# Out projection and values: the squares for the next norm run two slices later behind the residual rows' accumulating DMAs

## The chip, the cores and the metric

The kernel runs on one core of a Trainium2 chip. The time is the device time of one execution in microseconds, the median of several runs. The engines named below are PE (matrix products, with PEld for its weight loads), DVE (vector), ACT (scalar and activation), POOL (general) and SP, which here only issues DMAs. Each engine works through its own list of instructions strictly in order. A wait in that list holds up everything behind it on the same engine.

## The reference, cut to what matters

One transformer-like layer on 2048 tokens of width 1024, in float32. Between the sub-layers stand RMS norms, one behind each sub-layer before the residual is added (post) and one ahead of the next (pre):

```
y = concatenate([ya, yh]) @ w_out          # out projection
h = h + rms_norm(y, g_mix_post)            # residual row h1
u = rms_norm(h, g_x_pre)                   # only its 1/rms is needed as a factor of the scores
y = cross_attention(u, m, wq, wk, wv, wo)  # scores, softmax, values
h = h + rms_norm(y, g_x_post)              # residual row h2
u = rms_norm(h, g_ffn_pre)                 # input of the feed-forward
y = (silu(u @ w_gate) * (u @ w_up)) @ w_down
h = h + rms_norm(y, g_ffn_post)
```

So each row of the out projection and of the values is normed twice: its squares are summed, it is scaled, the residual is added, and the squares of the sum are summed again for the next norm.

## The kernel before, in words

The head of the program (input projection, windowed attention, the recurrence, and the folding of the cross-attention weights into two 1024 x 1024 matrices) takes the first 790 us and isn't touched. Then `phases` runs a chain of jobs, each a product of 2048 tokens with 1024 x 1024 matrices: the out projection (`mixed_block`), the scores (`score_block`), the values (`value_block`), gate and up of the feed-forward (`hidden_blocks`) and three parts of the down projection (`down_block`).

A job of these consists of eight blocks of 256 tokens (n = 0, 2, ... 14, counted in 128-token rows). A block multiplies by a scheme with seven instead of eight products of halves (`seven`). Each of the seven steps is one slice: 12 matrix products of 128 x 128 by 128 x 512, since every float32 operand is split into a high and a low part (`products`, lines 1032 to 1034). The two first and the two last blocks of a job run as pairs, slice by slice in turn; the middle four run one after the other. The token operands S are made from loaded tiles by `streamed` and `split2` (ACT line 896 or POOL line 898 for the high part, DVE line 899 for the low one) into five rotating buffers. The weight operands T are loaded through `row` tiles and split once per job. A product bank that isn't finished is copied by ACT into a `part` tile (line 1047) before it is used again.

When a quarter of a block (one of two rows of 128 tokens, one half of the width) is done, `out` adds it into a `row` tile (`squared`: DVE line 1391 or ACT line 1393) and sums its squares on ACT (`mean_square`, line 1369, profile name `junk`). What is still to be done with the block's two rows is written as a generator, `after`, which is appended to a list when the block's last slice has been recorded. From then on each slice of later blocks advances each `after` in the list by one `yield`. So a `yield` is one slice of distance in the order in which the program is recorded. A planner then orders each engine's list by its own estimate of times and by the dependencies, so the distance on the chip isn't exactly the recorded one.

In the two jobs of the change, `after` does the following, slice by slice: `rstds` on POOL (lines 1380, 1382, 1384: sum, epsilon, power -0.5), the scaling of each row on DVE (line 1417 or 1489), the residual added by an accumulating DMA issued by POOL (`add`, line 1398), the store of the residual row by SP (line 78, `h_d<-row`: the profile shortens h1_d and h2_d to this name); one slice of pause; the squares of each row's sum, two per row on ACT (`mean_squares`, line 1369); a second `rstds`. The out projection keeps its result in r_x (line 1426), transposes both rows on PE (`transposed`, line 1284, copied by ACT, line 1285) and stores them as h1t. The values scale each row again into a new `row` tile u on DVE (line 1500), transpose that and store it in u_d; for n = 4 and 6 sums of halves are also formed and stored (u_s). The row is transposed from, squared and stored only after the accumulating DMA has landed.

`row` tiles come from one pool of nine; the rows of T, the blocks' rows, u and the rows for the sums of the next job's weights share it.

Of the kernel before, what the change touches and what calls it, by code (L numbers as in the profile page):

```python
# [48 lines left out]
class Layer:  # L49
# [1350 lines left out]
    def mixed_block(self, n):  # L1400
        nc = self.nc
        y, ss = {}, []

        def out(i, j, a, b):
            if not y:
                ss.append(self.small("q_s", 4))
                if not n:
                    self.g_mix_post = self.gain(self.I["g_mix_post"])
            if i not in y:
                y[i] = self.row_tile()  # L1410
            self.squared(y[i][:, j * 512:(j + 1) * 512], a, b, ss[0][:, 2 * i + j:2 * i + j + 1])

        def after():
            r = self.rstds(ss[0])
            s2 = self.small("q_s", 4)
            for i in range(2):
                nc.vector.scalar_tensor_tensor(y[i], y[i], r[:, i:i + 1], self.g_mix_post, ALU.mult, ALU.mult)
                self.add(y[i], self.I["x"], n + i)
                self.store(self.h1_d[(n + i) * P:(n + i + 1) * P, :], y[i])
                yield  # L1420
            yield
            for i in range(2):
                self.mean_squares(y[i], i, s2)
                yield
            r = self.rstds(s2)
            nc.gpsimd.tensor_scalar(self.r_x[:, n:n + 2], r, 1.0, None, ALU.mult)
            yield
            for i in range(2):
                self.store(self.h1t_d[n + i], self.transposed(y[i], y[i]))
                yield  # L1430

        return self.tokens(self.y_d, n), out, after, None

    def score_block(self, n):
# [35 lines left out]
    def value_block(self, n):  # L1470
        nc = self.nc
        y, ss = {}, []

        def out(i, j, a, b):
            if not y:
                ss.append(self.small("q_s", 4))
            if i not in y:
                y[i] = self.row_tile()
                if n == 0 and len(y) == 1:
                    self.g_x_post = self.gain(self.I["g_x_post"])  # L1480
                    self.g_ffn_pre = self.extra_tile()
                    self.load(self.g_ffn_pre, self.I["g_ffn_pre"][0:1, :].broadcast_to([P, D]))
            self.squared(y[i][:, j * 512:(j + 1) * 512], a, b, ss[0][:, 2 * i + j:2 * i + j + 1])

        def after():
            r = self.rstds(ss[0])
            s2 = self.small("q_s", 4)
            for i in range(2):
                nc.vector.scalar_tensor_tensor(y[i], y[i], r[:, i:i + 1], self.g_x_post, ALU.mult, ALU.mult)
                self.add(y[i], self.h1_d, n + i)  # L1490
                self.store(self.h2_d[(n + i) * P:(n + i + 1) * P, :], y[i])
                yield
            yield
            for i in range(2):
                self.mean_squares(y[i], i, s2)
                yield
            r = self.rstds(s2)
            u = [self.row_tile() for _ in range(2)]
            for i in range(2):
                nc.vector.scalar_tensor_tensor(u[i], y[i], r[:, i:i + 1], self.g_ffn_pre, ALU.mult, ALU.mult)  # L1500
                yield
            o = []
            yield
            for i in range(2):
                tv = self.transposed(u[i], u[i])
                self.store_transposed(self.u_d, n + i, tv)
                if 4 <= n < 8:
                    o.append(self.row_tile().rearrange("p (k t) -> p k t", k=KT))
                    self.load(o[i], self.u_d[:, :, (n + i - 4) * P:(n + i - 3) * P].rearrange("k p t -> p k t"))
                yield  # L1510
            for i in range(len(o)):
                tv = u[i].rearrange("p (k t) -> p k t", k=KT)
                s = self.row_tile().rearrange("p (k t) -> p k t", k=KT)
                with self.behind():
                    nc.vector.tensor_tensor(s[:, 0:4], tv[:, 0:4], o[i][:, 0:4], ALU.subtract)
                    nc.vector.tensor_tensor(s[:, 4:8], tv[:, 4:8], tv[:, 0:4], ALU.subtract)
                yield
                with self.behind():
                    nc.vector.tensor_tensor(o[i][:, 0:4], o[i][:, 0:4], s[:, 4:8], ALU.add)
                    nc.vector.tensor_tensor(o[i][:, 4:8], o[i][:, 4:8], o[i][:, 0:4], ALU.subtract)  # L1520
                at = slice((n + i - 4) * P, (n + i - 3) * P)
                for c, t in enumerate((s[:, 0:4], s[:, 4:8], o[i][:, 0:4], o[i][:, 4:8])):
                    self.store(self.u_s[c][:, :, at], t)
                yield

        return self.tokens(self.pt_d, n), out, after, None

    def hidden_blocks(self, b, f):
# [137 lines left out]
```

## Time and profile before

| what | us |
|---|---|
| median of 3 runs (2600.45 to 2605.1) | 2603.19 |
| the profiled execution | 2603.6 |
| its span | 2601.7 |
| PE busy, share of the span | 2528.0, 97% |
| ACT busy | 1262.0 |
| DVE busy | 1746.0 |
| granted clock of PE, mean | 0.992 |

The span is the time from the first to the last instruction. A matrix product counts as busy from its issue to its end, and products overlap, so a busy share of 97% doesn't say that PE runs at its peak; what a change can win is read from the places where PE sits idle. In the profile's rows a bracket holds the idle time ahead of an instruction on its engine and what ended it. A granted clock below 1 means that PE was throttled for part of a stretch.

### The profile page before, as it was taken

Reading aid. Unit: us, or ns where it says so; the run is one execution under the profiler, and the core shown is the slowest. Engines: PE = TensorE matmul, PEld = TensorE weight load, DVE = VectorE, ACT = ScalarE, POOL = GpSimd, SP = SyncE. Lnnn points to the kernel's source line nnn. Section 1 sums busy time; section 2 is a strip of 40 time slices with the busy share of each in tenths; the row PEclk is TensorE's granted clock in tenths of the full one; section 3 lists DMA queues with packets and bytes.
Section 4 is the critical chain, followed back from the end, with each engine's and each line's share of the span. In section 5 each row is a group of like instructions: output and inputs, shape, how many; then the busy total and the mean of one; then the engine's idle time right before and its main releaser. Section 6 shows DMA issues by size and latency. Waiting matters only on the chain.

```text
span 2601.7 us, 34516 instructions
## 1 busy us (share of the span) xinstructions
PE 2528.0 (97%) x12160; PEld 2115.2 (81%) x12160; DVE 1746.0 (67%) x2773; ACT 1262.0 (49%) x2641; POOL 466.6 (18%) x651
## 2 busy tenths in 40 slices
PE   7989999999998999999999999999999999999998
PEld 6878788878997778888778888888888888888786
DVE  7675578887646568786785555576666656664756
ACT  5463366655654565565563333354333335443543
POOL 4240343320312224223320000000000000000022
PEclk9999999999999999999999999999999999999999
DMA  5434655484875998656984532353456434576798
GB/s 186 143 120 167 208 157 171 131 267 157 279 259 207 289 328 258 221 191 187 302 273 138 167 124 73 105 186 116 167 182 230 147 108 168 174 225 174 232 228 208
DMA packets 286350, 497.88 MB, mean 191 GB/s; under 512 B 20576, under 2 KB 143456, under 8 KB 286176
## 3 DMA queue, kind: packets, MB, share of 16 engines
q1 hardware_dynamic: 275520, 456.87, 52.3%
q0 software_dynamic: 10656, 38.80, 8.0%
q8 instruction: 96, 1.57, 0.2%
q14 instruction: 78, 0.64, 0.1%
HBM read 328.87 MB, written 166.72 MB: 190 GB/s over the span
## 4 chain that ended last, share of the span: by engine, by line
PE 80%; DMA 8%; DVE 4%; issue 3%; POOL 2%; ACT 2%; SPq 0%; DVEq 0%; POOLq 0%; ACTq 0%
PE psm L1032 22%; PE psm L1034 22%; PE psm L1033 22%; PE psg L163 2%; PE psg L164 2%; PE psg L165 2%; DMA row<-in_x_dram 1%; PE pss L1284 1%; DMA row<-h_d 1%; DMA u_d<-row 1%; DMA h_d<-row 1%; DMA x<-in_w_out_dram 1%; ACT junk L1369 1%; DMA pair<-in_x_dram 1%; DMA extra<-qk_d 0%
## 5 line engine op out<-in xcount | busy, mean ns | idle before, releaser
L1032 PE MATMUL psm<-T,S 128*128 128x512 f32 x2664 | 1036.4, 393 | 24.6 <-ACT S L896 13.8
L1033 PE MATMUL psm<-T,S 128*128 128x512 f32 x2664 | 1041.9, 391 | 0.0
L1034 PE MATMUL psm<-T,S 128*128 128x512 f32 x2664 | 1037.3, 392 | 2.6 <-DVE S L899 2.5
L1032 PEld LDWEIGHTS psm<-T,S 128*128 128x128 f32 x2664 | 503.3, 189 | 132.6 <-ACT S L896 15.1
L1034 PEld LDWEIGHTS psm<-T,S 128*128 128x128 f32 x2664 | 502.5, 189 | 109.2 <-DVE S L899 4.8
L1033 PEld LDWEIGHTS psm<-T,S 128*128 128x128 f32 x2664 | 503.2, 189 | 103.3
L896 ACT ACTIVATE S<-sum 128x512 fp32r<-128x512 f32 (+1 forms) x338 | 208.0, 619 | 340.1 <-PE psm L1034 331.7
L899 DVE TENSOR_TENSOR S<-sraw,S 128x512 fp32r<-128x512 f32 (+1 forms) x311 | 214.4, 697 | 224.4 <-ACT S L896 214.9
L899 DVE TENSOR_TENSOR S<-sum,S 128x512 fp32r<-128x512 f32 (+1 forms) x404 | 277.1, 690 | 84.3 <-ACT S L896 66.6
L1047 ACT ACTIVATE part<-psm 128x512 f32<-128x512 f32 x297 | 175.1, 592 | 174.9 <-PE psm L1034 168.0
L896 ACT ACTIVATE S<-sraw 128x512 fp32r<-128x512 f32 (+1 forms) x272 | 166.8, 617 | 154.7 <-PE psm L1034 143.1
L1398 POOL DMA_DIRECT2D row<-y_d x28 | 25.0, 892 | 1131.4 <-DMA sraw<-hid_d 964.8
L1369 ACT ACTIVATE junk<-row 128x512 f32<-128x512 f32 x160 | 99.7, 624 | 121.8 <-DVE row L1391 33.4
L899 DVE TENSOR_TENSOR T<-row,T 128x1024 fp32r<-128x1024 f32 x104 | 123.0, 1190 | 28.7 <-ACT T L896 28.5
L163 PE MATMUL psg<-u,whi 128*128 128x512 f32 x352 | 141.2, 401 | 1.0 <-POOL whi L145 1.0
L165 PE MATMUL psg<-u,wlo 128*128 128x512 f32 x352 | 139.5, 396 | 1.5 <-DVE wlo L146 1.5
L164 PE MATMUL psg<-u,whi 128*128 128x512 f32 x352 | 139.6, 397 | 0.0
L896 ACT ACTIVATE T<-row 128x1024 fp32r<-128x1024 f32 x104 | 105.8, 1027 | 23.7 <-DMA row<-in_w_down_dram 10.9
L146 DVE TENSOR_TENSOR wlo<-raw,whi 128x1024 fp32r<-128x1024 f32 x54 | 68.8, 1275 | 33.2 <-ACT whi L143 26.6
L898 POOL TENSOR_SCALAR S<-sum 128x512 fp32r<-128x512 f32 x66 | 49.0, 742 | 234.7 <-PE psm L1034 141.0
L1550 DVE TENSOR_TENSOR part<-psm,part 128x512 f32<-128x512 f32 x66 | 45.4, 688 | 64.6 <-PE psm L1034 64.5
L1541 DVE TENSOR_TENSOR row<-psm,part 128x512 f32<-128x512 f32 x66 | 45.5, 689 | 57.4 <-PE psm L1034 57.3
(329 smaller groups left out, 3644.3 us busy)
## 6 DMA issues: line engine op xcount, KB each, us to landing
sraw<-in_w_gate_dram SPq DMA_DIRECT2D x44, 512.0 KB, 4.9
sraw<-in_w_up_dram SPq DMA_DIRECT2D x44, 512.0 KB, 4.8
hid_d<-row SPq DMA_DIRECT2D x44, 512.0 KB, 2.7
h_d<-row SPq DMA_DIRECT2D x32, 512.0 KB, 6.9
y_d<-row SPq DMA_DIRECT2D x32, 512.0 KB, 3.6
sraw<-hid_d SPq DMA_DIRECT2D x32, 512.0 KB, 5.2
row<-h_d POOLq DMA_DIRECT2D x30, 512.0 KB, 8.1
row<-y_d POOLq DMA_DIRECT2D x28, 512.0 KB, 7.3
```

Source lines behind the costliest of these rows:

```text
L146: nc.vector.tensor_tensor(lo, raw, f32(hi), ALU.subtract)
L163: nc.tensor.matmul(ps, ah, bh, start=(i == 0), stop=False)
L164: nc.tensor.matmul(ps, ah, bl, start=False, stop=False)
L165: nc.tensor.matmul(ps, al, bh, start=False, stop=(i == n - 1))
L896: self.nc.scalar.activation(hi, raw, AF.Copy)
L898: self.nc.gpsimd.tensor_scalar(hi, raw, 1.0, 1.0, ALU.mult, ALU.mult)
L899: self.nc.vector.tensor_tensor(lo, raw, f32(hi), ALU.subtract)
L1032: nc.tensor.matmul(ps, s[:, 0, k, :], t[:, 0, k, :], start=st, stop=False, **kw)
L1033: nc.tensor.matmul(ps, s[:, 0, k, :], t[:, 1, k, :], start=False, stop=False, **kw)
L1034: nc.tensor.matmul(ps, s[:, 1, k, :], t[:, 0, k, :], start=False, stop=sp, **kw)
L1047: nc.scalar.activation(t, ps, AF.Copy)
L1369: self.nc.scalar.activation(junk, a, AF.Square, scale=float(D) ** -0.5, accum_out=to)
```

## The change

In `mixed_block` and in `value_block` the pause between the slice that issues the second row's residual add and the slice with the first row's squares grows from one `yield` to three. Everything behind it in `after` (squares, second `rstds`, second scaling, transposes, stores of h1t or u) is recorded two slices later. Nothing is added, removed or computed differently. `down_block`, which has a similar pause, stays as it was.

```
@@ mixed_block, after
                 self.add(y[i], self.I["x"], n + i)
                 self.store(self.h1_d[(n + i) * P:(n + i + 1) * P, :], y[i])
                 yield
-            yield
+            for _ in range(3):
+                yield
             for i in range(2):
                 self.mean_squares(y[i], i, s2)
                 yield
@@ value_block, after
                 self.add(y[i], self.h1_d, n + i)
                 self.store(self.h2_d[(n + i) * P:(n + i + 1) * P, :], y[i])
                 yield
-            yield
+            for _ in range(3):
+                yield
             for i in range(2):
                 self.mean_squares(y[i], i, s2)
                 yield
```

More of the change, by code (lines that the diff above doesn't have):

```diff
@@ L1420, in after @@
                 yield
-            yield
+            for _ in range(3):
+                yield
             for i in range(2):
@@ L1492, in after @@
                 yield
-            yield
+            for _ in range(3):
+                yield
             for i in range(2):
```

## The prediction

> **What bounds the kernel now.** I read the page first, then the busy time by windows, then the idle stretches of PE in its timeline, then who waits for what around the line that moves.
>
> ```profile
> span 2601.7 us, 34516 instructions
> PE 2528.0 (97%) x12160; PEld 2115.2 (81%) x12160; DVE 1746.0 (67%) x2773; ACT 1262.0 (49%) x2641; POOL 466.6 (18%) x651
> PE 80%; DMA 8%; DVE 4%; issue 3%; POOL 2%; ACT 2%; SPq 0%; DVEq 0%; POOLq 0%; ACTq 0%
> L1369 ACT ACTIVATE junk<-row 128x512 f32<-128x512 f32 x160 | 99.7, 624 | 121.8 <-DVE row L1391 33.4
> ```
>
> PE carries 80% of the chain, so a change elsewhere counts only where PE waits for it, and through the clock that it finds after a wait. The windows show where that is (columns: PE, PEld, DVE, ACT and POOL busy, granted clock, DMA share, GB/s):
>
> ```profile
> 880.00:900.00 20.00, 17.60 (x79) 14.70 (x80) 11.99 (x15) 11.53 (x28) 6.22 (x11) 0.91 0.92 301
> 920.00:940.00 20.00, 17.06 (x73) 13.78 (x72) 8.81 (x13) 8.92 (x23) 4.76 (x9) 0.91 0.97 287
> 980.00:1000.00 20.00, 17.98 (x84) 14.79 (x84) 16.12 (x20) 10.72 (x26) 11.38 (x17) 0.98 0.88 219
> 1000.00:1020.00 20.00, 20.00 (x94) 16.52 (x93) 16.92 (x25) 13.10 (x33) 6.91 (x11) 0.94 1.00 345
> 1020.00:1170.00 150.00, 150.00 (x723) 125.14 (x722) 123.66 (x226) 91.28 (x213) 34.76 (x48) 1.00 0.60 202
> 1290.00:1310.00 20.00, 17.23 (x67) 13.25 (x66) 15.06 (x18) 13.46 (x27) 5.37 (x8) 0.83 1.01 306
> 1330.00:1350.00 20.00, 15.75 (x68) 12.81 (x68) 16.22 (x20) 12.58 (x28) 5.24 (x8) 0.93 0.96 258
> 1350.00:2601.00 1251.00, 1239.29 (x5473) 1024.56 (x5471) 772.86 (x1137) 506.10 (x895) 51.08 (x69) 1.00 0.53 167
> ```
>
> Scores (1020 to 1170) keep PE full at clock 1.00, and the 1251 us of the feed-forward lose 12 us in all. The holes lie in the two jobs that the diff touches, the out projection (about 790 to 990) and the values (about 1165 to 1345), with the DMA share near 1. PE's idle stretches there, in brackets with the releaser:
>
> ```profile
> 878.70 0.39 PE L1033 MATMUL psm<-T,S 128*128 128x512 f32 x1
> 878.93 0.39 PE L1034 MATMUL psm<-T,S 128*128 128x512 f32 x1
> 882.40 1.34 PE L1284 MATMUL pss<-ident,row 128*128 128x128 f32 x8 [2.40 <-DMA row<-in_x_dram]
> 884.40 0.63 PE L1033 MATMUL psm<-T,S 128*128 128x512 f32 x1
> 884.82 0.63 PE L1034 MATMUL psm<-T,S 128*128 128x512 f32 x1
> 910.21 0.47 PE L1032 MATMUL psm<-T,S 128*128 128x512 f32 x1 [1.39 <-DVE row L1391]
> 930.10 1.26 PE L1284 MATMUL pss<-ident,row 128*128 128x128 f32 x8 [2.94 <-DMA row<-in_x_dram]
> 999.00 1.92 PE L1284 MATMUL pss<-ident,row 128*128 128x128 f32 x8 [2.02 <-ACT row L1285]
> 1281.47 1.06 PE L1284 MATMUL pss<-ident,row 128*128 128x128 f32 x8 [1.42 <-DVE row L1500]
> 1299.94 0.79 PE L1032 MATMUL psm<-T,S 128*128 128x512 f32 x1 [2.65 <-ACT S L896]
> 1347.62 0.79 PE L1032 MATMUL psm<-T,S 128*128 128x512 f32 x1 [4.25 <-ACT S L896]
> ```
>
> Products follow each other every 0.23 us before a hole and every 0.42 us for some time behind it (878.70/878.93 against 884.40/884.82). A slice is 12 products, so 12 x 0.23 = 2.8 us, and a block of 7 slices with its 16 transposes about 21 us.
>
> The six holes other than that at 910.21 have one root: the residual row's accumulating DMA hasn't landed when something in order behind it comes up.
>
> ```profile
> 865.52 0.60 ACT L1393 ACTIVATE row<-psm 128x512 f32<-128x512 f32 x1 [1.31 <-PE psm L1034]
> 882.37 0.63 ACT L1369 ACTIVATE junk<-row 128x512 f32<-128x512 f32 x1 [8.03 <-DMA row<-in_x_dram]
> 886.79 0.62 ACT L1369 ACTIVATE junk<-row 128x512 f32<-128x512 f32 x1
> 907.60 0.63 ACT L1369 ACTIVATE junk<-row 128x512 f32<-128x512 f32 x1 [3.14 <-DMA row<-in_x_dram]
> 912.06 0.62 ACT L1369 ACTIVATE junk<-row 128x512 f32<-128x512 f32 x1
> 930.07 0.63 ACT L1369 ACTIVATE junk<-row 128x512 f32<-128x512 f32 x1 [8.49 <-DMA row<-in_x_dram]
> 935.20 0.62 ACT L1369 ACTIVATE junk<-row 128x512 f32<-128x512 f32 x1
> 1337.67 0.64 ACT L1369 ACTIVATE junk<-row 128x512 f32<-128x512 f32 x1 [6.35 <-DMA row<-h_d]
> ```
>
> ```profile
> ACT junk L1369 <- DMA row<-in_x_dram: 32.0, 9, 8.5
> ACT junk L1369 <- DMA row<-h_d: 29.4, 9, 6.3
> 867.29 0.19 POOL L1380 TENSOR_TENSOR q_v<-q_s 128x2 f32<-128x2 f32 x1 [1.10 <-ACT junk L1369]
> 867.87 0.71 POOL L1384 TENSOR_TENSOR q_r<-q_w,mhalf 128x2 f32<-128x2 f32 x1
> 873.09 0.94 POOL L1398 DMA_DIRECT2D row<-in_x_dram  x1 [4.51 <-DVE row L1417]
> DMA to landing us min/median/max: 5.5/10.0/12.7
> DMA to landing us min/median/max: 5.3/10.0/13.3
> ```
>
> A block's last product is copied at 865.52, its add is issued at 873.09 and lands 9.3 us later, at 882.37. ACT stood before that row's square for 8.03 us. Over both jobs ACT loses 32.0 + 29.4 = 61.4 us like this, with the products' S tiles (line 896) and bank copies (line 1047) behind it. Landings (the last two lines: the adds of x, then of h1) have a median of 10.0 us.
>
> **The change part by part.** No instruction is added, removed or reshaped. Of each block's `after`, everything behind the adds comes two slices later: per block four squares on ACT, the second `rstds` on POOL (3 operations, in the out projection also r_x), 16 transposes on PE with four ACT copies, the store of h1t or u on SP, and in the values two scalings on DVE, in two pairs of blocks also the sums u_s. The adds and the h1/h2 stores keep their slice. Built and set side by side, the two programs differ so:
>
> ACT. In the middle blocks 20 to 26 activations, where there were 12 to 16, stand between a block's last own square and its next-norm square. The first norm square now comes right behind the next block's square of its third quarter, the second row's behind that of its last. In the old times those third-quarter squares ran at 886.79, 912.06 and 935.20, against landings at 882.37, 907.60 and 930.07: 4.4, 4.5 and 5.1 us of slack where ACT waited 8.0, 3.1 and 8.5. At the ends of the jobs the squares gain only a few activations: 17 becomes 18 in the out projection, 21 becomes 22 in the values for the first row of the pair. There I expect part of the wait to stay.
>
> POOL. It is in order, and it now has the second `rstds` of a block immediately ahead of the first `rstds` of the next, whose scaling and add follow. That add therefore waits for two more squares, 2 x 0.62 = 1.25 us, and shares POOL with a second chain, about 0.19 + 0.71 us and a short operation between, some 1.3 us: 2.6 us later. The slack above falls to about 2 us at a median landing and is gone at 12.7. The S tiles of line 898 that stand behind it are covered: with five S buffers they are made four slices ahead, 4 x 2.8 = 11 us.
>
> PE. The transposes wait for the row itself. In the block after 865.52 the first one stood 50 products behind the block's last product and now stands 66 behind it, so 16 x 0.23 = 3.7 us later, against a hole of 2.40. At 930.10 the shift is 1.5 slices against 2.94 us plus the later add: just enough.
>
> SP. The h1 and h2 stores still wait for each landing with the loads of later blocks behind them, as before. Only the h1t and u stores drop behind a load or two, and their readers are blocks of the next job. The row pool (9 tiles) holds each y two slices longer, 2 x 2 rows x 2.8 us per 21 us block, about half a tile more on average. I cost that at nothing: in the middle of a job no T is loaded, and at its ends ACT waits little for a row of T:
>
> ```profile
> ACT T L896 <- DMA row<-qk_s: 2.1, 1, 2.1
> ACT T L896 <- DMA row<-u_s: 2.1, 2, 1.9
> ```
>
> None of this reaches PE. If that cover goes, SP stands before a load whose row isn't free, and the sum is off by a hole of the size above for each such load.
>
> The sum, against the profiled execution's 2603.6 us (span 2601.7), which is 0.4 above the median of 2603.2:
> - Idle of the six holes: 2.40 + 2.94 + 2.02 + 1.42 + 2.65 + 4.25 = 15.7 us.
> - Clock behind them, 20 us times the part not granted in the windows at 880, 920, 980, 1000, 1290 and 1330: 1.8 + 1.8 + 0.4 + 1.2 + 3.4 + 1.4 = 10.0 us. So 25.7 us is all that there is to win, 2578.
> - Inside the jobs I take all: 2.40 + 1.8 + 2.94 + 1.8 + 1.42 = 10.4, and 2.65 + 3.4 = 6.1 at 1299.94, whose S tile moves ahead of the squares that held it. Of the two job ends (2.02 + 1.6 and 4.25 + 1.4 = 9.3) I take half, 4.6. That is 21.1.
> - Against it new waits that before doesn't show. Their lower bound is 0. The upper bound for one is a hole like 882.40's, 2.40 + 1.8 = 4.2, at each of 10 places (four middle blocks and one end per job), 42. With slack of about 2 us and landings that spread 5 to 13, I take a short wait at about two of ten, rounded down to 7 us.
>
> Net 14 us: 2603.6 - 14 = 2589.6, so 2590.
>
> The clock term rests on rows: behind the hole of 2.40 us products come at 0.42 us. [...]
>
> **The rivals.**
> - All waits behind the adds go, and nothing new comes: 2603.6 - 25.7 = 2578. For it, the slack in the middle blocks; against it, the few activations gained at the job ends.
> - Nothing is won. In the holes' windows the DMA share is 0.88 to 1.01, so the transfers may set the pace: PE comes to the same wait with another instruction, and it is 2603. Against it, the window at 1000 moves 345 GB/s beside 287 in that of the hole of 2.94 us, so there is room. [...]
> - Slower: the squares now stand straight ahead of the copies that free a product bank, and POOL's next add behind them. If a landing slips past the slack, ACT stops with no S tile in hand and the next block's add is late as well. The price is 2.02 + 1.6 = 3.6 us (the hole at 999.00) at each of the ten places, 36 - 25.7 = 10 us more: 2614. It decides from a median landing of about 12 us, where 10.0 is seen; half of the ten places would need it.
>
> **How the numbers follow.** Forecast 0.55 (its own range 2581 to 2597), all won 0.13, nothing won 0.15, slower 0.17. About 0.2%, 5 us, can be told from no change. Faster by more: 0.55 + 0.13 less a little of the forecast's edge, 0.67. Within: 0.14, from the rival that wins nothing. Slower: 0.17 and an edge of that rival, 0.19. The range runs from just below the ceiling, 2577, to 2606, and leaves out most of the slower case.
>
> **What would show it.** Right: ACT's wait of the squares for the two row DMAs falls from 61.4 us to under 20; no transpose of line 1284 waits for a row's DMA; the windows at 880, 920 and 1290 show clock 1.00; the end near 1347 keeps some idle time. Wrong: landings with a median over 12 us; PE released by line 1047 or 1393 behind a square; POOL's line 1380 followed by late adds; or a T tile waiting for its row.

## The result, and the profile after

The changed kernel takes 2616.57 us (median; 2613.56 to 2628.49) beside 2603.06 us for the kernel before. The ratio is 1.0053, with a 95% interval from 1.0041 to 1.0064: slower by 13.5 us. The profiled execution took 2613.56 us. The page of the changed kernel:

```profile
span 2611.9 us, 34504 instructions
PE 2527.6 (97%) x12160; PEld 2114.8 (81%) x12160; DVE 1746.1 (67%) x2773; ACT 1262.9 (48%) x2641; POOL 463.8 (18%) x651
L1032 PE MATMUL psm<-T,S 128*128 128x512 f32 x2664 | 1037.2, 393 | 34.4 <-ACT part L1047 20.7
L1369 ACT ACTIVATE junk<-row 128x512 f32<-128x512 f32 x160 | 99.6, 625 | 73.3 <-DVE row L1391 38.2
```

The squares' idle time ahead (line 1369) fell from 121.8 to 73.3 us, and no engine has more work. Yet the span grew by 10.2 us, and the first products of a group (line 1032) now wait above all for ACT's bank copies of line 1047. The long stretches of idle PE between 840 and 1370 us, in PE's timeline of the changed kernel:

```profile
868.14 0.50 PE L1032 MATMUL psm<-T,S 128*128 128x512 f32 x1 [0.69 <-ACT part L1047]
873.16 0.50 PE L1034 MATMUL psm<-T,S 128*128 128x512 f32 x1 [1.10 <-DVE S L899]
913.99 1.15 PE L1284 MATMUL pss<-ident,row 128*128 128x128 f32 x8 [1.32 <-ACT row L1285]
916.79 0.50 PE L1032 MATMUL psm<-T,S 128*128 128x512 f32 x1 [1.65 <-ACT part L1047]
938.84 1.14 PE L1284 MATMUL pss<-ident,row 128*128 128x128 f32 x8 [1.82 <-ACT row L1285]
955.02 1.06 PE L1284 MATMUL pss<-ident,row 128*128 128x128 f32 x8 [1.38 <-DMA row<-in_x_dram]
957.83 0.50 PE L1032 MATMUL psm<-T,S 128*128 128x512 f32 x1 [1.75 <-ACT S L896]
1003.53 0.80 PE L1034 MATMUL psm<-T,S 128*128 128x512 f32 x1 [3.24 <-DVE S L899]
1220.78 0.50 PE L1034 MATMUL psm<-T,S 128*128 128x512 f32 x1 [1.02 <-DVE S L899]
1243.95 0.50 PE L1032 MATMUL psm<-T,S 128*128 128x512 f32 x1 [1.56 <-ACT part L1047]
1266.69 0.50 PE L1032 MATMUL psm<-T,S 128*128 128x512 f32 x1 [1.57 <-ACT part L1047]
1306.53 0.50 PE L1032 MATMUL psm<-T,S 128*128 128x512 f32 x1 [3.31 <-ACT part L1047]
1318.93 0.47 PE L1032 MATMUL psm<-T,S 128*128 128x512 f32 x1 [2.32 <-ACT part L1047]
1357.24 0.79 PE L1032 MATMUL psm<-T,S 128*128 128x512 f32 x1 [2.40 <-ACT part L1047]
```

The seven old holes were 17.1 us together; of these only that at the end of the values has a counterpart with the same releaser (4.25 us before; 1.55 and 0.88 us now, at 1352.50 and 1354.12, not in the list). The fourteen in the list are 25.1 us. In all, PE stood idle for 27.6 us between 840 and 1370 us, where it had been 18.7. Seven of the fourteen, 0.69 + 1.65 + 1.56 + 1.57 + 3.31 + 2.32 + 2.40 = 13.5 us, are released by line 1047 (that this equals the loss of time is chance: the sum holds neither the holes that went nor the clock). Who waits for what on ACT (out projection, 840 to 1010 us, three lines; then values, 1170 to 1370 us):

```profile
ACT S L896 <- PE psm L1034: 25.5, 7, 6.7
ACT junk L1369 <- DVE row L1391: 17.2, 6, 7.4
ACT junk L1369 <- DMA row<-in_x_dram: 6.5, 4, 2.3
...
ACT S L896 <- PE psm L1034: 40.8, 14, 6.7
...
ACT junk L1369 <- DMA row<-h_d: 1.1, 1, 1.1
```

The waits behind the adds are nearly gone: 6.5 + 1.1 = 7.6 us in these windows, where the two rows of before had 61.4. They weren't what PE had to pay. What took their place is seen at a block's end. ACT in the kernel before, in the middle of the values:

```profile
1235.21 0.60 ACT L1393 ACTIVATE row<-psm 128x512 f32<-128x512 f32 x1 [1.26 <-PE psm L1034]
1235.71 0.62 ACT L896 ACTIVATE S<-sum 128x512 fp32r<-128x512 f32 x1
1236.23 0.62 ACT L1369 ACTIVATE junk<-row 128x512 f32<-128x512 f32 x1
...
1236.84 0.59 ACT L1047 ACTIVATE part<-psm 128x512 f32<-128x512 f32 x1
```

and in the changed one, at the same block:

```profile
1240.84 0.60 ACT L1393 ACTIVATE row<-psm 128x512 f32<-128x512 f32 x1 [2.19 <-PE psm L1034]
1241.47 0.63 ACT L1369 ACTIVATE junk<-row 128x512 f32<-128x512 f32 x1
...
1242.10 0.61 ACT L1369 ACTIVATE junk<-row 128x512 f32<-128x512 f32 x1
...
1242.71 0.61 ACT L1369 ACTIVATE junk<-row 128x512 f32<-128x512 f32 x1
...
1243.33 0.57 ACT L1047 ACTIVATE part<-psm 128x512 f32<-128x512 f32 x1
```

The block's last quarter is copied (1393) and squared (the first 1369). Before, an S tile and that square lay between this and the next block's bank copy: the copy starts 1.63 us behind the start of line 1393. Now the second row's two squares of the next norm lie there too, 1242.10 and 1242.71, and the copy starts 2.49 us behind it. They wait for nothing; they are just 2 x 0.61 us of work. But behind the block's last product (1240.41) PE's list had only seven products, the last of them at 1242.00. Then PE stood for 1.56 us, until the copy freed the bank.

That PE had so little in hand comes from the change as well. Both programs' lists, read beside their traces, show it. In the kernel before, PE's timeline has 15 products and 8 transposes between that block's last product (1234.79) and the first into the bank that the copy frees:

```profile
1239.31 0.39 PE L1032 MATMUL psm<-T,S 128*128 128x512 f32 x1
```

The copy was done at 1237.43, with 1.88 us to spare, so 0.86 us more would have cost nothing. The planner, which orders PE's list too, has now put five products of the next block ahead of this block's last slice. In three other middle blocks of the changed kernel (copies at 891.69, 942.01 and 1289.14) the same squares stand ahead of the copy and PE doesn't stop, since it has 12 products or more in hand. So the stall takes both: the squares ahead of the copy, and a PE list with little behind the block's last product. The stalls at 868.14 and 1266.69 have the same three squares alone ahead of the copy; that at 916.79 has a wait of ACT for an h1 store there too:

```profile
913.34 1.09 ACT L1285 ACTIVATE row<-pss 128x512 f32<-128x512 f32 x2 [1.97 <-DMA h_d<-row]
```

The stall of 3.24 us at 1003.53, at the end of the out projection, has another root. Its S tile stands on DVE behind line 943, which combines weights for the values and waits for their load (first line: before; the others: changed):

```profile
999.95 1.22 DVE L943 TENSOR_TENSOR extra<-extra,g 128x1024 f32<-128x1024 f32 x1 [3.20 <-DMA g<-vo_d]
...
1001.64 1.22 DVE L943 TENSOR_TENSOR extra<-extra,g 128x1024 f32<-128x1024 f32 x1 [4.22 <-DMA g<-vo_d]
1002.79 0.68 DVE L899 TENSOR_TENSOR S<-sum,S 128x512 fp32r<-128x512 f32 x1
```

### The profile page after: what moved, and what is told of

The parts are those of the page before. It is cut to its first block, busy times and chain, and to the rows that moved or that the text cites. A ratio compares the mean times of both kernels' runs of the same rounds, so it can differ in the third digit from the quotient of the medians.

```text
span 2611.9 us, 34504 instructions
## 1 busy us (share of the span) xinstructions
PE 2527.6 (97%) x12160; PEld 2114.8 (81%) x12160; DVE 1746.1 (67%) x2773; ACT 1262.9 (48%) x2641; POOL 463.8 (18%) x651
## 3 DMA queue, kind: packets, MB, share of 16 engines
q8 instruction: 96, 1.57, 0.2%
## 5 line engine op out<-in xcount | busy, mean ns | idle before, releaser
L1369 ACT ACTIVATE junk<-row 128x512 f32<-128x512 f32 x160 | 99.6, 625 | 73.3 <-DVE row L1391 38.2
L898 POOL TENSOR_SCALAR S<-sum 128x512 fp32r<-128x512 f32 x66 | 54.8, 831 | 239.7 <-PE psm L1034 149.6
```

Of the source, the lines that this page charges most:

```text
L898: self.nc.gpsimd.tensor_scalar(hi, raw, 1.0, 1.0, ALU.mult, ALU.mult)
L1369: self.nc.scalar.activation(junk, a, AF.Square, scale=float(D) ** -0.5, accum_out=to)
```

## The experiments

Three readings were set against each other at first: that S tiles which wait for PE stand ahead of the copies on ACT (A); that POOL's two chains make each next add late (B); and, after A's run, that the squares' own work stands ahead of the copies (C). Later came the job ends (D) and what follows the squares (E). All ratios are to the kernel before.

### Which of the two jobs loses

The run named e1 was meant to hold the out projection's change alone. By a slip it held that of the values, so it is the same program as e2, and its expectation doesn't apply to it; e5 is what e1 should have been.

```
 e2, and by the slip e1: values three yields, out projection as before
 e5: out projection three yields, values as before
-            yield
+            for _ in range(3):
+                yield
```

> Only the out projection's squares are two slices later; the values keep the order of before. Followed instruction by instruction, the profiled runs put about 2 to 3 of the 10 us of span that were lost into the out projection and about 6 into the values. If the loss is local to each job, this kernel takes 2603 + 3 = 2606 us (2603 to 2608). Rival: the loss comes through what both jobs share (row tiles, SP's order of loads, the list order of what follows); then the two kernels with one half each don't add up to 13 us, and this one may be as slow as 2612 or not slower at all.

> Only the values' squares are two slices later. Local loss: 2603 + 6 to 10 = 2609 to 2613 us, with the stalls of PE behind the copies of line 1047 at about 1306 and 1357 us still there. Rival (shared cause): no sum of the two halves to 13 us.

> Three slices between adds and squares in the out projection alone; the values keep the order of before. (The kernel run under the name e1 had by a slip the values' change in it, as e2.) The values alone measured 2614, 8 to 9 us over before. If the losses are local to the jobs, the out projection alone has the rest of the 13.5 us: 2606 to 2609 us. If the two share a cause, or if any new list order loses as much, it takes 2612 us or more, too.

The values alone: 1.0034 (1.0022 to 1.0045) as e1 and 1.0032 (1.0021 to 1.0043) as e2, 8 to 9 us. The out projection alone: 1.0012 (1.0001 to 1.0023), 3 us. Their sum, 12 us, agrees with the 13.5 of both, as it would if the loss is local to each job, with about two thirds of it in the values. The two profiles of the same program (e1, e2) have spans of 2616.6 and 2612.0 us, so a difference of that size between two profiles means little; the ratios decide.

### Is it the S tiles that wait for PE? (A)

```
-            self.split2(src, t[:, 0], t[:, 1], engine or e)
+            with (self.behind() if self.pin else contextlib.nullcontext()): self.split2(...)
     # behind(): not ahead of the last ACT and DVE instruction of the current slice
     # pin: in the out projection and the values
```

> As the changed kernel, but in the out projection and the values each S tile's split is held on ACT and DVE behind the copies and squares of the slice before which it is recorded, so that none can stand ahead of a bank copy. Theory A expects ACT's waits of S tiles for PE (25.5 us in the out projection, 40.8 in the values) to fall to under 20 together, PE's waits for line 1047 to go, and the loss with them: 2603 us or less, down to 2592 if the waits for the adds that the change took away count as well. Theory B expects no gain: 2614 us or more. If S tiles now come too late, PE waits for line 896 and it is slower than 2617.

1.0213 (1.0193 to 1.0232), 55 us slower than before. The waits that A blames did go: in the changed kernel S tiles waited for PE 25.5 + 40.8 us, and in this one that row isn't in either job's list. PE's side instead (out projection, then values):

```profile
PE psm L1032 <- ACT S L896: 8.4, 5, 3.0
...
PE psm L1032 <- ACT part L1047: 8.3, 4, 5.8
PE psm L1032 <- ACT S L896: 8.1, 5, 2.1
```

S tiles that are made early wait, but they are in hand when PE needs them; made late they make PE wait: 16.5 us for line 896, against 1.7 + 2.4 = 4.1 us in the changed kernel (840 to 1010 and 1170 to 1370 us). A isn't borne out: with those waits gone PE still waits 10.7 us for line 1047 (2.4 in the out projection), against 13.5 in the changed kernel, and in the rows at 1240 to 1243 above no S tile stands ahead of the copy. What the 66 us of waits cost by themselves the run can't say, since it brings waits of its own.

### Is it POOL's pair of chains? (B)

```
                 self.mean_squares(y[i], i, s2)
                 yield
+            yield
             r = self.rstds(s2)
```

> As the changed kernel, but the second rstds of a block comes one slice later still, so that POOL no longer has it straight ahead of the next block's first rstds and its add (the transposes are one slice later too). Theory A (ACT's list: S tiles that wait for PE stand ahead of bank copies) expects no gain, 2614 to 2619 us, and line 1047 still as PE's releaser. Theory B (the pair on POOL makes every next add 2.6 us late, and the rest follows from that) expects adds about 2.6 us nearer to the block's own squares and most of the loss back: 2603 to 2608 us.

1.0076 (1.0062 to 1.009), 20 us slower than before. The adds did move: in the values' middle blocks a first row's add comes 12 to 15 us behind that row's last own square, where it came 15 to 19 in the changed kernel, and a second row's 6 to 8 where it was 10 to 14. But nothing came back: it is slower than the changed kernel. So B isn't supported, and ACT's 7.6 us of waits for the adds speak against it as well. The run doesn't exclude a small gain, since it also sets the second `rstds` and all behind it one slice later, which has a price (e13 below).

### Is it the squares in front of the bank copy? (C)

```
 e6: both rows' squares in one slice, rest as in the changed kernel
             for i in range(2):
                 self.mean_squares(y[i], i, s2)
-                yield
+            yield
+            yield

 e7: the second row's squares one slice later, behind the copy
                 self.mean_squares(y[i], i, s2)
                 yield
+                yield
```

> As the changed kernel, but the second row's squares are recorded in the slice of the first row's, one earlier; rstds, transposes and all else keep their slice. In the changed kernel's list the second row's two squares stand, in seven or eight blocks, between the block's last own square and the next block's first bank copy, where PE has only about six products (1.4 us) in hand: idle of 0.69, 1.65, 1.56 and 1.57 us behind line 1047 at 868, 917, 1244 and 1267 us. Theory C (the work of the squares, 2 x 0.62 us, in front of that copy) expects these four stalls gone, so 5.5 us or more back: 2611 us or less. Theory D (the loss sits at the ends of the jobs, where T rows and S tiles meet the late squares) expects no gain: 2614 to 2619. If squares of a row that hasn't landed now make ACT wait, line 1369 waits for the adds by over 15 us, and the time is over 2617.

> As the changed kernel, but the second row's squares one slice later, so that they stand behind the next block's first bank copy (and rstds and transposes one slice later with them). Theory C expects the same four stalls to go: 2611 us or less. Theory D, or a cost that comes from rstds and transposes being late, expects 2617 to 2624, as with the kernel whose rstds alone came one slice later (2624).

e6: 1.0029 (1.0019 to 1.0039). Six of the 13.5 us came back, where C had said 5.5 or more. ACT at the same block's end in e6:

```profile
1240.53 0.60 ACT L1393 ACTIVATE row<-psm 128x512 f32<-128x512 f32 x1 [1.14 <-PE psm L1034]
1241.16 0.63 ACT L1369 ACTIVATE junk<-row 128x512 f32<-128x512 f32 x1
1241.80 0.58 ACT L1047 ACTIVATE part<-psm 128x512 f32<-128x512 f32 x1
```

The copy is back at 1.27 us behind line 1393, and of the four stalls none is left: PE's waits for line 1047 in the values fell from 11.2 to 0.4 us (this takes in the stalls at the job's end, some of which only changed their releaser). That fits C's reading of the stalls. That these four were worth 6 us isn't shown. In e6 PE's list also has 11 products and 8 transposes behind this block's last product, where the changed kernel has 7, so the run doesn't separate the squares from the products in hand; and the table at the end of this section finds the time that came back at another place.

e7: 1.0093 (1.0078 to 1.0109), the opposite of what C had said of the time. Three of the four stalls are gone (the one of 0.69 us is left), and in the out projection's window PE is busy for 216.1 us, more than before's 213.2. The loss is in two holes at the end of the values:

```profile
1310.22 1.94 PE L1284 MATMUL pss<-ident,row 128*128 128x128 f32 x8 [7.37 <-DVE row L1504]
1321.68 0.79 PE L1032 MATMUL psm<-T,S 128*128 128x512 f32 x1 [9.52 <-ACT part L1047]
```

The first are transposes of u that wait for DVE's scaling to u (line 1500 in the kernel before): the tail behind the squares. So C isn't all, and what follows the squares has a price of its own in the values.

### The ends of the jobs, and the row tiles (D)

```
 e8: the last two blocks of both jobs keep one yield
-            for _ in range(3):
+            for _ in range(1 if n >= NT - 4 else 3):

 e9 (from the changed kernel), e10 (from the kernel before)
-  tag="row", ..., bufs=9        self.raws, self.parts, self.sums = 6, 4, 5
+  tag="row", ..., bufs=10       self.raws, self.parts, self.sums = 6, 4, 3
```

> As the changed kernel, but the last two blocks of each of the two jobs keep the one slice of before. Theory D expects most of the loss back, 2603 to 2608 us: the stalls at 1003.5 (3.24 us), 1306 (3.31), 1319 (2.32) and 1354 to 1357 (3.3) go back to before's 2.0, 2.65 and 4.25. Theory C expects the four stalls of the middle blocks to stay, and so 2610 us or more.

> The changed kernel with 10 row tiles instead of 9 (and 3 sum tiles instead of 5, which makes the room). At the end of the values the first T rows of the feed-forward are loaded into row tiles that u and its sums leave two slices later; their loads came at 1311 us behind two h2 stores, against 1291 us ahead of them before, ACT waited 5.08 us for one, and PE 3.31 and 2.32 us behind it. If late row tiles are the cause, these two stalls shrink, and this kernel is 4 to 6 us nearer to its partner with before's slices and 10 rows than the 13.5 us that stand between the kernels with 9 rows. If not, the difference stays 11 to 16 us.

> The partner: the kernel before with 10 row tiles and 3 sum tiles. If neither count matters for the order of before, 2601 to 2607 us; fewer sum tiles may cost a few us, the same in both.

e8: 1.0036 (1.0022 to 1.0051). Its interval overlaps the changed kernel's, so what the last blocks are worth isn't settled; between nothing and 9 us. Its four stalls of the middle blocks stayed, as C had it.

e9: 1.0029 (1.002 to 1.0038); e10: 1.0037 (1.0023 to 1.0051). With ten row tiles there is no difference between the two orders. But this isn't the gain that was expected: e10 is itself 10 us slower than the kernel before, and the stall that more row tiles should have shrunk has grown. In e9 it is

```profile
1310.39 0.77 PE L1032 MATMUL psm<-T,S 128*128 128x512 f32 x1 [8.00 <-ACT part L1047]
```

So the row tiles aren't shown to be the cause, but the pair doesn't exclude them either: it changes two counts at once. In their profiles, counted as in the table below, e9 and e10 lose 3.9 and 4.8 us behind 2300 us, in the last part of the down projection, where the changed kernel loses 0.8. Whether fewer sum tiles cost this directly, or by the list order that they lead to, wasn't tried.

### What follows the squares, alone (E)

```
 e13: from the kernel before, values only
                 self.mean_squares(y[i], i, s2)
                 yield
+            for _ in range(2):
+                yield
             r = self.rstds(s2)
 e14: e6, and in the values
-            for _ in range(3):
+            for _ in range(1 if 4 <= n < 8 else 3):
```

> The kernel before, with only what follows the next-norm squares in the values (rstds, scalings to u, transposes, u stores, the sums of u) two slices later; all squares of both jobs and the out projection as before. Theory E (that tail is late where the feed-forward's first T rows come, and costs PE there) expects stalls of 3 us or more between 1300 and 1325 us behind lines 1047 or 1504, and 2608 to 2614 us. If lateness of the squares alone is what costs, nothing changes: 2602 to 2607 us.

> As the kernel with both rows' squares in one slice (2611, 6 us better than the changed one), but in the values the two blocks whose u goes into the sums of u keep the one slice of before. Theory E expects the late sums, and with them the stalls at about 1268 (3.88 us in that kernel) and 1308 (2.44), to shrink: 2603 to 2608 us. If the sums have no part in it, 2609 to 2613 us.

e13: 1.0024 (1.0015 to 1.0034), 6 us slower, with every square where it was before. So the tail alone (second `rstds`, scaling to u, transposes, stores and sums) has a price in the values. Its place isn't quite the expected one, 1300 to 1325 us:

```profile
1265.73 1.07 PE L1284 MATMUL pss<-ident,row 128*128 128x128 f32 x8 [3.85 <-DVE row L1502]
```

Transposes that stand in PE's list wait for DVE's scaling to u (line 1502 here). The longest such hole before was that of 1.42 us at 1281.47. A hole of 4.36 us at 1354.10, behind line 1047, is no longer than the 4.25 us that before shows at the end of the values.

e14: 1.0015 (1.0004 to 1.0027), lower than e6 by 0.0014, with overlapping intervals: the sums of u may have a part in it, which the run doesn't settle.

### Is there a distance that is better than before?

```
 e12: both jobs            e11: out projection         e15: as e11, n < NT - 4
-  yield                  -  yield                    (last two blocks as before)
+  for _ in range(2):     +  for _ in range(3):
+      yield              +      yield
                             ... second row's squares one yield later
                             values as before
```

> The out projection with three slices between adds and squares and the second row's squares one later still, behind the next block's bank copy; the values as before. In the kernel that had this in both jobs the out projection (790 to 1020 us) kept PE busy for 216.1 us, against 213.2 before, and its stalls fell, while the values lost. Theory C (the squares' work in front of the bank copy is what the out projection lost) expects 2599 to 2604 us, so no slower than before and 4 us or more better than the out projection alone with two slices (2609). If later is simply worse, 2610 us or more.

> Two slices between adds and squares in both jobs, so one later than before instead of two. No square stands between a block's last own square and the bank copy in the middle blocks. Theory C expects no stall behind line 1047 there and less loss than with two slices: 2600 to 2610 us, with some of ACT's waits for the adds back (15 to 35 us of the 61). If loss grows evenly with lateness, 2608 to 2612 us and stalls of line 1047 at about half their size.

> The out projection with three slices before the squares and the second row one later still (2605.5 in both ends and middle), but its last two blocks as before, and the values as before. That kernel lost 2.9 us in the scores' first 60 us and about 1.2 us at 1017, behind the last blocks' late squares. With these as before: 2599 to 2603 us, 2 to 5 us under the kernel before. If the end of the job then gets its old holes back (2.0 us at 999, and the clock behind it), 2604 to 2606.

e12, one slice later: 1.0015 (1.0003 to 1.0026), 4 us slower, under a third of the loss at two slices. No square stands ahead of the copies in its middle blocks, ACT's waits for the adds are 27.3 us, as expected, and it has one stall of 3.04 us behind line 1047 (at 876.62) that wasn't. e11: 1.0001 (0.9991 to 1.0011). With the second row's squares behind the copy the out projection isn't slower than before; that this is better than e5 isn't shown, since the intervals overlap. e15: 0.9999 (0.999 to 1.0009), no gain either. No order tried here beats the kernel before; but e11 and e15 show that a new list order need not lose either.

### Where the time lies, product by product

Every trace holds 8556 products of lines 1032 to 1034. The start of the k-th product, less that of the k-th in the kernel before, is the lag of a run at that point. The table has how much the lag grew in each stretch (us; times are those of the kernel before, and a minus is a gain).

| run | out projection, 790 to 1000 | its end, 1000 to 1060 | values, 1170 to 1290 | their end, 1290 to 1400 |
|---|---|---|---|---|
| changed kernel | -3.1 | 5.2 | 1.0 | 5.2 |
| e5, out projection alone | -3.5 | 7.5 | 2.4 | -2.1 |
| e15, its middle alone, later | -7.0 | 6.7 | 0.4 | -1.1 |
| e2, values alone | 1.5 | 0.1 | 1.0 | 4.2 |
| e1, the same program as e2 | -1.6 | 1.6 | 1.0 | 10.1 |
| e6, squares together | -1.9 | 7.2 | 3.2 | -1.5 |
| e13, values' tail alone | -0.1 | 0.9 | 3.4 | 1.6 |

These are single profiles: in the first 790 us, which no edit touches, their lags already differ from -0.6 to 5.9 us (7.6 in e4), and e1 and e2 differ by 5.9 us at the end of the values. But one thing holds in all eleven runs with a later out projection (e4 left out): its middle gains 1.3 to 7.0 us, and its end loses 3.6 to 8.6. So a gain in the middle of this job, as was forecast, did come, and was lost at the job's end, in the changed kernel behind the load at 1001.64. e10, whose squares aren't later, shows the same (4.1 gained, 7.8 lost), so lateness isn't the only thing that brings it about. And e6 lost more than the changed kernel in the two middles, where the four stalls were, and less at the end of the values.

## Why the prediction was wrong, point by point

- **The waits behind the adds** were to fall from 61.4 us to under 20. Right: 7.6 us.
- **PE's transposes** were no longer to wait for the row's DMA. Right but for one, 1.38 us at 955.02, at the end of the job, where part of the wait was expected to stay.
- **The clock**: 1.00 was expected in the windows at 880, 920 and 1290. Right for 880 and 920, and the old holes are gone. At 1290 it is 0.92. But new holes brought new stretches below 1.00 (the windows with the lowest clocks; columns as before):

```profile
1000.00:1020.00 20.00, 16.76 (x76) 13.66 (x75) 14.25 (x21) 11.21 (x27) 4.57 (x10) 0.91 0.94 319
1300.00:1320.00 20.00, 14.37 (x60) 11.27 (x59) 13.67 (x20) 11.71 (x24) 5.09 (x7) 0.91 0.98 281
1340.00:1360.00 20.00, 15.17 (x60) 11.51 (x59) 19.98 (x26) 16.40 (x33) 7.93 (x11) 0.87 1.05 297
```

These three alone are 1.8 + 1.8 + 2.6 = 6.2 us of the 10.0 that were to be won.
- **POOL's pairing** was to make the next add 2.6 us late. The direction was right, the size too small, and no cost of it is seen: the block whose add came 10.6 us behind its first row's last own square now has it 14.9 us behind, yet ACT waits 7.6 us in all. The squares had more slack than the 2 us worked out.
- **The step that failed** is the term "Against it new waits that before doesn't show ... I take 7 us". The holes that are new by their instruction and releaser measure 25.1 us, the fourteen listed above. The term was sized only as waits for landings, by slack and spread, and only one of the fourteen (1.38 us) was released by a landing. Over half of the idle time, 13.5 us, is behind bank copies. The prediction had seen that the second row's squares now come behind the next block's last square, and in its rival that they stand ahead of the copies that free a bank, but it costed the squares there only if they had to wait. Their own work, 1.22 us, was costed at nothing, and so was the new order of PE's list, which at the block shown left seven products in hand where there had been 15 with 8 transposes. Three stalls, 0.69 + 1.56 + 1.57 = 3.8 us, show this with nothing else in ACT's way, and a fourth of 1.65 us behind an h1 store as well. What they are worth in time stays open: e6 took them away and came 6 us nearer, but not at their places.
- **The ends of the jobs** were to win 4.6 us, half of their holes and of the clock behind them. By the table they lost 5.2 us each. In the out projection, PE comes sooner to the end and stands behind the load at 1001.64. For the values the runs show the place but no single wait.
- **The tail in the values.** The prediction names the second scalings and the sums among what comes later, gives them no term, and ends its costing of the stores and the row tiles with "None of this reaches PE." In the values the tail alone costs 6 us (e13). The 6 us of e6 and these 6 us would be most of the 13.5, but no run shows that they are two separate parts. By which wait the tail costs at the end of the values, T rows behind stores on SP or DVE's scalings ahead of the next block's, stays open. The changed kernel shows an instance of the first, ACT's 5.08 us ahead of the stall at 1318.93, where the prediction had "at its ends ACT waits little for a row of T" and named a T tile waiting for its row as a sign of being wrong:

```profile
1310.62 0.33 SPq L78 DMA_DIRECT2D h_d<-row  x1
1311.05 1.24 SPq L75 DMA_DIRECT2D row<-u_d  x2
...
1317.24 1.06 ACT L896 ACTIVATE T<-row 128x1024 fp32r<-128x1024 f32 x1 [5.08 <-DMA row<-u_d]
1318.21 0.58 ACT L1047 ACTIVATE part<-psm 128x512 f32<-128x512 f32 x1
```

The load of a T row is issued right behind an h2 store, which waits for its row's add to land (issued at 1301.59, landed at 1310.60), and a bank copy stands behind the T tile.
- **The rivals.** The slower one gave 2614, near the 2616.6 measured, and has one place right, the copies; that its number is near is luck, for its condition isn't what decided. It asked for a median landing of about 12 us; the adds of x, then those of h1, land in the two jobs' windows of the changed kernel after

```profile
DMA to landing us min/median/max: 5.5/10.0/12.5
DMA to landing us min/median/max: 5.5/7.8/10.6
```

so no slower than before. That the DMAs set the pace doesn't explain the three stalls: ACT waits for no transfer there. At the end of the out projection it may be right, "PE comes to the same wait with another instruction": the load at line 943 held DVE for 3.20 us before and 4.22 us after, and the middle's gain was lost there. No run took this load away.

## What to carry to other kernels

Work that is moved behind a wait still has to run somewhere: look at what stands directly behind its new place in the engine's list (here a bank copy, which started 2.49 us behind line 1393 instead of 1.63), and how much the bounding engine has in hand at that moment. Look for that in the changed program, not in the old one: where a planner orders the lists, the cushion moves as well (here from 15 products and 8 transposes to seven products, 1.6 us, against 1.22 us of squares). The size of a wait on an engine off the critical path says little of what its removal wins: 53.8 of 61.4 us of waits went, and the kernel became slower. What follows the moved piece counts as part of the move: here the tail alone cost 6 us. And a gain in the middle of a stage counts only if the stage's end doesn't wait for something else (here 1.3 to 7.0 us gained in the out projection's middle and 3.6 to 8.6 lost at its end): set the runs side by side product by product, not hole by hole.

## What the runs showed of the hardware that was not expected

The clock behind a hole doesn't go by the hole's length alone. A hole of 2.32 us (1318.93 above) was followed by products 0.23 us apart (granted clock 1.00 from 1320 to 1325), while one of 2.19 us (884.04 in e13) was followed by products 0.43 us apart until 887.9 (0.91 from 880 to 900). In e15 the products were 0.23 us apart at first (956.68, 956.91), and the slow pace began 1.2 us behind the end of the hole (PE's timeline there):

```profile
956.37 0.47 PE L1032 MATMUL psm<-T,S 128*128 128x512 f32 x1 [2.83 <-ACT part L1047]
...
957.60 0.60 PE L1034 MATMUL psm<-T,S 128*128 128x512 f32 x1
958.00 0.63 PE L1032 MATMUL psm<-T,S 128*128 128x512 f32 x1
...
961.25 0.39 PE L1032 MATMUL psm<-T,S 128*128 128x512 f32 x1
```

It lasted from 957.6 to 961.0, 3.4 us, with products 0.43 us apart (958.00, 958.43), behind a hole of 2.83 us. What sets its start and its length no run here shows.
